# Holding back the part-array products of a recurrent layer and issuing them with a step of the recurrence, sorted by shape

## The chip, the core and the metric

One core of a Trainium2 chip runs one launch of the kernel. The metric is the device time of that launch in microseconds (us), lower is better. The engines are called TensorE (PE in the rows, its weight loads PEld), VectorE (DVE), ScalarE (ACT), GpSimd (POOL) and SyncE (SP, which issues the DMAs).

## What is computed

One layer of a hybrid encoder over 512 prompt frames and 32 sample frames, 544 in all, in fp32. A normalised input goes through one input projection; sixteen heads of stick-breaking attention and sixteen heads of an RWKV-7 recurrence work on its columns; their outputs are concatenated and go through one output projection; then a gated FFN follows.

```python
proj = rms_norm(x, norm1_g) @ w_in
q, k, v, xr = split(proj)
o = rms_norm(stick_breaking(q, k, v))
y_r, S_T = rwkv7_mix(xr, shift0, S0)
x = x + concat([o, y_r]) @ w_out
x = x + conv_ffn(rms_norm(x, norm2_g))
...
def step(S, inp):
    sa = einsum('bhvk,bhk->bhv', S, -kk_t)
    S = S * w_t + sa * (kk_t * a_t) + v_t * k_t
    return S, einsum('bhvk,bhk->bhv', S, r_t)
```

## The kernel before

Heads are worked in pairs: a pair's two 64-wide heads lie on the 128 partitions. There are 8 pairs of recurrence heads (blocks 8 to 15 of the output projection's input) and 8 pairs of attention heads (blocks 0 to 7).

**Main products.** `project` and `part` multiply the input, split into a high and a low fp32r part (`xh`, `xl`), by weights that are split likewise after their DMA (`wr` raw, `wh` and `wl` split). For one block of 128 rows that is six matmuls of 128x272, issued by `products` (L376) into a PSUM tile `pj`, of which there are two. A column block of the input projection is 96 such matmuls. I call these the full products; they fill the array.

**Side work.** Everything of the heads runs as Python generators ("threads") that are stepped while the program is recorded. `products` calls `tick` (L130) three times per block; `tick` steps each thread whose `wake` is not past the model's clock `clk["PE"]`; a thread issues a few instructions and yields. `charge` (L75) keeps the model's clock of each engine in ns, from a fixed cost and a cost per column. The clock only decides the order in which instructions are recorded; on the chip each engine runs its own list in order and waits by semaphores. `until` (L141) advances the clock by 100 at a time with nothing issued on TensorE but side work, until a condition holds. `get` and `gets` hand out buffers; for a PSUM bank (`ps`, four of them) a thread may take one before it is free in the model and then yields until it is.

**Part-array products.** Many products of the side work use a part of the array: 64 or 32 rows, or 64 or 32 columns of it. In `rwkv` (L761) these are the decay gates (`sigms`, 64 rows), the chunk products `ps<-AR,TH` (64x128), the block inverse (64x64 and 32x32). In `rwkv_chain` (L944) they are the recurrence itself: for each pair 8 steps, each of three products that depend on each other through a copy or a multiply-add on ScalarE or VectorE:

```python
mm(q[R[h], ...], AM[h][:, c, 0:C], XV[h][:, c, 0, :], ...)   # ps<-XV,AM  128x64
mm(q[R[h], ...], c3(MI)[R[h], c, :], ru[R[h], ...], ...)     # ps<-ru,w   64x64
mm(q[R[h], ...], BK[:, c, R[h]], XV[h][:, c, 1, :], ...)     # ps<-XV,BK  128x64
```

After the last step follow the output products (64x64 and 128x64, `ps<-AR,XV` and `ps<-AM,XV`), a normalisation, the gate, and `deliver` (L692), which splits the result for the output projection or parks it in DRAM (`ocat`). A pair's chain cannot start before the one before has given back `XV` and `BK`, of which there is one each.

**Output projection.** After the last input column block, the loop `while m in OUT` (L1525) makes output column blocks while heads are still being worked. The first takes its input blocks in the order `EARLY` (L1522):

```python
EARLY = [[8, 9, 10, 11], [0, 1, 2, 3], [12, 13, 4, 5]]
...
until(lambda: all(k in oh for k in g))
part(ps, oh, ol, g, ...)
```

so its third group needs the recurrence pairs 4 and 5 (blocks 12 and 13). A block made before all heads are done is parked (`part_out`, L1503) and finished later. When all threads are done (L1551) the side buffers are given back and the FFN's buffers `q` take their place; the residual rows and the rest of the weights are loaded into them.

Of the kernel before, what the change touches and what calls it, by code (L numbers as in the profile page):

```python
# [41 lines left out]
def hymba_step(ctx: ExitStack, tc: tile.TileContext, A: dict, O: dict):  # L42
# [21 lines left out]
    clk = {e: 0.0 for e in COST}  # L64
    threads = []
    cur = [None]

    class Thread:
        def __init__(self, g, first):
            self.g, self.first, self.wake, self.rd = g, first, clk["PE"], {}  # L70

# [54 lines left out]
    def spawn(g, first=False):  # L126
        n = sum(th.first for th in threads)
        threads.insert(n if first else len(threads), Thread(g, first))

    def tick():  # L130
        for th in list(threads):
            if th.wake <= clk["PE"]:
                cur[0] = th
                try:
                    next(th.g)
                    th.wake = th.ready()
                except StopIteration:
                    threads.remove(th)
                cur[0] = None

# [30 lines left out]
    FREE = {}  # L171
    POOLS = {}
# [17 lines left out]
    def gets(tag, n, dtype=F32):  # L190
        while len(FREE[tag]) < n:
            yield
        ts = [alloc(tag, POOLS[tag][2], dtype) for _ in range(n)]
        yield from settle()
        return ts

    def getm(tag, shape=None, dtype=F32):
# [506 lines left out]
    def sigms(p, S, lw2):  # L704
        names = ("w0", "a0")
        bias = [par[name][:, p:p + 1] for name in names]
        ems = []
        for _ in names:
            x = yield from gets("w", 2)
            ems.append(x)  # L710
        for s in HALVES:
            qs = yield from gets("ps", 2)
            for q, r in zip(qs, R):
                mm(q[:, :HT], lw2[r, :], lin[r, s], True, True)
            yield
            for q, b, (e, m) in zip(qs, bias, ems):
                act(e[:, s], q[:, :HT], AF.Abs, bias=b)
                V.tensor_scalar(m[:, s], q[:, :HT], b, 0.0, op0=ALU.add, op1=ALU.min)
            put(*qs)
        yield  # L720
        spawn(sigm(S, "a0", *ems[1]))
        yield from sigm(S, "w0", *ems[0])
# [38 lines left out]
    def rwkv(p, S):  # L761
# [60 lines left out]
        for c0 in range(0, NC_, 4):  # L822
            n = min(4, NC_ - c0)
            qs = yield from gets("ps", 2)
            for c in range(n):
# [74 lines left out]
        for a_, b_ in CH:  # L900
            q = yield from get("ps")
            v, s = prod(q, NA, MT, a_, b_)
            yield
            AC.copy(GA[:, s], v)
            put(q)
        put(NA)
        for a_, b_ in CH:
            yield
            q = yield from get("ps")
            v, s = prod(q, GA, M, a_, b_)  # L910
# [9 lines left out]
        E_ = [slice(64 * h + 32, 64 * h + 64) for h in range(2)]  # L920
        q = yield from get("ps")
        q3 = q[:, 0:NC_ * 32].rearrange("p (c t) -> p c t", t=32)
# [8 lines left out]
        yield  # L931
        q = yield from get("ps")
        q3 = q[:, 0:NC_ * 32].rearrange("p (c t) -> p c t", t=32)
# [10 lines left out]
    def rwkv_chain(p, S):  # L944
# [52 lines left out]

        q = yield from get("ps")
        tr(q[:, :64], stin[0:64, :], ident[0:64, 0:64])
# [7 lines left out]
        for i in range(8):  # L1007
# [4 lines left out]
            yield  # L1012
            q = yield from get("ps")
            for u, c in enumerate(cl):
# [6 lines left out]
            yield  # L1021
            q = yield from get("ps")
            for u, c in enumerate(cl):
# [7 lines left out]
            yield  # L1031
            q = yield from get("ps")
            for u, c in enumerate(cl):
# [13 lines left out]
        for a, b in [(0, 5), (5, 9)]:  # L1047
            q = yield from get("ps")

# [12 lines left out]

        q = yield from get("ps")
        for u in range(2):
# [216 lines left out]
    def attn_sample(p, S, D):  # L1281
# [43 lines left out]
        yield  # L1325
        q = yield from get("ps")
        for h in range(2):
# [1028 lines left out]
```

## Time and profile before

| what | value |
|---|---|
| median of 3 runs | 2681.56 us (2681.29 to 2681.99) |
| profiled execution | 2680.7 us, its span 2679.0 us |
| TensorE busy | 2644.4 us, 99% of the span |
| VectorE, ScalarE, GpSimd busy | 73%, 50%, 9% |
| granted clock of TensorE, mean | 0.998 |

A busy TensorE here is one with a matmul under way; a matmul's end is modelled and overlaps the next one, so costs are read from the distance between starts, not from durations. The heads are worked in the first 1120 us, the FFN takes the rest.

### The profile page before, as it was taken

Reading aid. Unit: us, or ns where it says so; the run is one execution under the profiler, and the core shown is the slowest. Engines: PE = TensorE matmul, PEld = TensorE weight load, DVE = VectorE, ACT = ScalarE, POOL = GpSimd, SP = SyncE. Lnnn points to the kernel's source line nnn. Section 1 sums busy time; section 2 is a strip of 40 time slices with the busy share of each in tenths; the row PEclk is TensorE's granted clock in tenths of the full one; section 3 lists DMA queues with packets and bytes.
Section 4 is the critical chain, followed back from the end, with each engine's and each line's share of the span. In section 5 each row is a group of like instructions: output and inputs, shape, how many; then the busy total and the mean of one; then the engine's idle time right before and its main releaser. Section 6 shows DMA issues by size and latency. Waiting matters only on the chain.

```text
span 2679.0 us, 54701 instructions
## 1 busy us (share of the span) xinstructions
PE 2644.4 (99%) x21978; PEld 2524.2 (94%) x21978; DVE 1968.8 (73%) x3573; ACT 1345.0 (50%) x2632; POOL 238.7 (9%) x609
## 2 busy tenths in 40 slices
PE   8999999999999999999999999999999999999999
PEld 7988898888888888999999999999999999999998
DVE  6676776667666754446878888887888887787887
ACT  5555665666656465434544444444444454343443
POOL 3210110101011100021010101001010100000000
PEclk9999999999999999999999999999999999999999
DMA  5222222222222243462354333434434364565653
GB/s 193 85 69 62 77 66 75 59 79 66 67 68 75 68 121 94 132 209 73 114 136 112 104 112 108 124 113 117 112 103 120 107 204 141 166 206 151 197 164 90
DMA packets 492968, 304.01 MB, mean 113 GB/s; under 512 B 45290, under 2 KB 458346, under 8 KB 492714
## 3 DMA queue, kind: packets, MB, share of 16 engines
q1 hardware_dynamic: 491434, 296.06, 38.3%
q8 instruction: 172, 2.82, 0.4%
q0 software_dynamic: 1280, 4.46, 0.4%
q14 instruction: 82, 0.67, 0.1%
HBM read 253.30 MB, written 47.16 MB: 112 GB/s over the span
## 4 chain that ended last, share of the span: by engine, by line
PE 93%; DVE 4%; ACT 2%; issue 1%; DMA 1%; SPq 0%; DVEq 0%; ACTq 0%
PE ps L216 35%; PE pj L216 29%; PE pt L216 27%; PE ps L220 1%; DVE w L109 1%; DVE q L109 1%; ACT w L109 1%; DVE wl L109 1%; ACT wh L109 0%; DMA xr<-in_x_prompt 0%; DVE sp L109 0%; ACT sp L109 0%; DVE xl L109 0%; DVE TH L109 0%; SPq L124 0%
## 5 line engine op out<-in xcount | busy, mean ns | idle before, releaser
L216 PE MATMUL pj<-xh,wh 128*128 128x272 f32 x1846 | 535.7, 305 | 9.0 <-ACT wh L109 4.4
L216 PE MATMUL pj<-xl,wh 128*128 128x272 f32 x1846 | 505.5, 289 | 0.3 <-DVE xl L109 0.3
L109 DVE TENSOR_TENSOR q<-q,q 128x1024 f32<-128x1024 f32 (+7 forms) x466 | 473.1, 1036 | 5.8 <-ACT q L109 2.7
L216 PE MATMUL pj<-xh,wl 128*128 128x272 f32 x1846 | 434.9, 306 | 5.9 <-DVE wl L109 5.9
L216 PEld LDWEIGHTS pj<-xh,wh 128*128 128x128 f32 x1846 | 349.6, 189 | 25.2 <-ACT wh L109 5.9
L216 PEld LDWEIGHTS pj<-xl,wh 128*128 128x128 f32 x1846 | 349.5, 189 | 4.1 <-issue 1.7
L109 DVE TENSOR_TENSOR wl<-wr,wh 128x512 fp32r<-128x512 f32 (+2 forms) x299 | 212.9, 714 | 184.5 <-ACT wh L109 176.7
L109 ACT CAST wr<-q 128x512 fp32r<-128x512 f32 (+1 forms) x301 | 180.9, 614 | 306.6 <-DVE q L109 217.3
L216 PEld LDWEIGHTS pj<-xh,wl 128*128 128x128 f32 x1846 | 298.0, 189 | 26.2 <-DVE wl L109 8.4
L109 ACT CAST wh<-wr 128x512 fp32r<-128x512 f32 (+2 forms) x299 | 181.6, 610 | 189.0 <-PE pj L216 95.4
L216 PE MATMUL ps<-xh,q 128*128 128x272 f32 x922 | 241.2, 289 | 0.0
L216 PE MATMUL ps<-q,q 128*128 128x272 f32 x1160 | 237.5, 289 | 0.0
L216 PE MATMUL pt<-xh,q 128*128 128x272 f32 x1038 | 233.4, 288 | 0.0
L216 PE MATMUL pt<-q,q 128*128 128x272 f32 x844 | 215.7, 289 | 0.0
L109 DVE TENSOR_TENSOR q<-q,wr 128x512 fp32r<-128x512 f32 (+1 forms) x301 | 201.0, 676 | 0.5 <-ACT wr L109 0.4
L216 PEld LDWEIGHTS ps<-q,q 128*128 128x128 f32 x1160 | 180.9, 188 | 0.3 <-ACT f L109 0.3
L216 PEld LDWEIGHTS pt<-xh,q 128*128 128x128 f32 x1038 | 174.5, 188 | 0.0
L216 PEld LDWEIGHTS ps<-xh,q 128*128 128x128 f32 x922 | 165.3, 188 | 0.0
L109 ACT CAST q<-q 128x1024 fp32r<-128x1024 f32 (+5 forms) x200 | 149.4, 765 | 26.2 <-DVE q L109 20.9
L109 ACT CAST wh<-q 128x512 fp32r<-128x512 f32 (+1 forms) x190 | 114.4, 602 | 70.7 <-PE ps L216 34.0
L216 PEld LDWEIGHTS pt<-q,q 128*128 128x128 f32 x844 | 147.9, 188 | 0.0
L216 PE MATMUL pt<-xl,q 128*128 128x272 f32 x520 | 141.7, 289 | 0.0
(323 smaller groups left out, 6248.9 us busy)
## 6 DMA issues: line engine op xcount, KB each, us to landing
wr<-in_w_in SPq DMA_DIRECT2D x200, 256.0 KB
q<-in_w_ffn_up SPq DMA_DIRECT2D x84, 512.0 KB
q<-in_w_ffn_gate SPq DMA_DIRECT2D x80, 512.0 KB
q<-in_w_ffn_down SPq DMA_DIRECT2D x48, 512.0 KB
hd<-f SPq DMA_DIRECT2D x44, 272.0 KB
q<-hd SPq DMA_DIRECT2D x22, 544.0 KB
wr<-in_w_ffn_down SPq DMA_DIRECT2D x44, 256.0 KB
q<-in_w_ffn_down SPq DMA_DIRECT2D x24, 384.0 KB
```

What stands on the lines that cost most here:

```text
L109: return f(*a, **kw)
L216: nc.tensor.matmul(out, lhsT, rhs, start=start, stop=stop, skip_group_check=True)
L220: nc.tensor.transpose(out, in_, ident)
```

## The change

`get("ps")` becomes `banks_for(shape)` at thirteen places, all of part-array products. Such a thread yields the name of a shape, and `tick` does not step it with the others. The letter ahead says whether it is a step of the recurrence ("c") or not ("s"). When a "c" thread is ready, or a thread has been ready for more than `PATIENCE` = 8000 ns of the model's clock, all ready threads of this kind are stepped in one go, sorted by the rest of the name. A bank is now taken only when it is free in the model.

```diff
+    def step(th):
+        cur[0] = th
+        try:
+            th.part = next(th.g)
+            th.wake = th.ready()
+        except StopIteration:
+            threads.remove(th)
+        cur[0] = None
+
+    PATIENCE = 8000
+
     def tick():
         for th in list(threads):
-            if th.wake <= clk["PE"]:
...
+            if th.wake <= clk["PE"] and not th.part:
+                step(th)
+        small = [th for th in threads if th.part and th.wake <= clk["PE"]]
+        if any(th.part[0] == "c" or clk["PE"] > th.wake + PATIENCE for th in small):
+            for th in sorted(small, key=lambda th: th.part[1:]):
+                step(th)
...
+    def banks_for(shape, n=1):
+        while True:
+            yield shape
+            if sum(t <= clk["PE"] for t in FREE["ps"][:n]) == n:
+                return [alloc("ps", POOLS["ps"][2]) for _ in range(n)]
...
-            qs = yield from gets("ps", 2)
+            qs = yield from banks_for("s64x128", 2)
...
-            q = yield from get("ps")
+            q, = yield from banks_for("c128x64")
...
-            q = yield from get("ps")
+            q, = yield from banks_for("c64x64")
...
-        q = yield from get("ps")
+        q, = yield from banks_for("s32x32")
```

No instruction's shape changes and both programs hold the same 20283 matmuls; what moves is their order, on every engine, from the first pair on. Three places follow.

**TensorE, the last chunk product of a pair.** `pj` is a full product, `ps<-AR,TH` the chunk product (64 rows of the array), `ps<-XV,BK` the third product of a recurrence step (64 columns). Before, of pair 7:

```order
L216 MATMUL pj_11467<-xh_343,wh_11468 128x272
L216 MATMUL pj_11467<-xl_352,wh_11468 128x272
L216 MATMUL ps_11550<-AR_10925,TH_11210 128x128
L216 MATMUL ps_11551<-AR_10925,TH_11210 128x128
L216 MATMUL pj_11467<-xh_343,wh_11468 128x272
```

Now, of pair 6, behind the first step of pair 5's chain:

```order
L234 MATMUL pj_11715<-xh_11909,wl_11973 128x272
L234 MATMUL ps_12054<-XV_1684_11074,BK_10784 64x64
L234 MATMUL ps_12054<-XV_1686_11082,BK_10784 64x64
L234 MATMUL ps_12054<-XV_1684_11074,BK_10784 64x64
L234 MATMUL ps_12054<-XV_1686_11082,BK_10784 64x64
L234 MATMUL ps_12059<-AR_11075,TH_11465 128x128
L234 MATMUL ps_12060<-AR_11075,TH_11465 128x128
L234 MATMUL pj_11715<-xh_11956,wh_11972 128x272
```

The chunk product stood alone between full products; now it stands behind a step of the recurrence, in the same gap of the full products.

**TensorE, the first output column block.** `XV,AM`, `ru,w` and `XV,BK` are the three products of a step. Before, the chain under way is that of pair 7, the last one:

```order
L216 MATMUL pj_12825<-xh_12644,wh_12834 128x272
L216 MATMUL pj_12825<-xl_12645,wh_12834 128x272
L216 MATMUL ps_12922<-XV_1918_12142,AM_1784_11369 64x64
L216 MATMUL ps_12922<-XV_1919_12143,AM_1793_11423 64x64
L216 MATMUL pj_12825<-xh_12644,wh_12834 128x272
L216 MATMUL pj_12825<-xl_12645,wh_12834 128x272
L216 MATMUL pj_12825<-xh_12644,wl_12835 128x272 x2
```

Now it is that of pair 5, and ahead of the block's third group there are no full products:

```order
L234 MATMUL pj_11715<-xh_11956,wl_11973 128x272 x2
L234 MATMUL ps_12081<-XV_1684_11074,AM_1534_10196 64x64
L234 MATMUL ps_12081<-XV_1686_11082,AM_1542_10230 64x64
L234 MATMUL ps_12093<-ru_12085,w_11157 64x64 x2
L234 MATMUL ps_12102<-XV_1684_11074,BK_10784 64x64
L234 MATMUL ps_12102<-XV_1686_11082,BK_10784 64x64
L234 MATMUL ps_12109<-XV_1684_11074,AM_1534_10196 64x64
L234 MATMUL ps_12109<-XV_1686_11082,AM_1542_10230 64x64
```

The chain's products follow each other without a full product between them; 297 matmuls of the side work stand here before the next `pj` row.

**VectorE, the same place.** `XV` rows are the chain's copies and multiply-adds, `sp` and `w` other side work, `wl` the split of the next weights. Before:

```order
L109 TENSOR_TENSOR wl_12835<-wr_12832,wh_12834 128x512
L109 SCALAR_TENSOR_TENSOR XV_1918_12142<-XV_1918_12142,pc_10921,ps_12815 64x64
L109 SCALAR_TENSOR_TENSOR XV_1919_12143<-XV_1919_12143,pc_10921,ps_12815 64x64
L109 COPY ts_12798<-ps_12823 128x128
L109 TENSOR_TENSOR wl_12899<-wr_12838,wh_12898 128x512
L109 TENSOR_TENSOR AM_2060_12907<-w_11476,AM_2060_12907 64x512
L109 COPY w_12936<-ps_12873 52x128
```

Now:

```order
L109 COPY XV_1686_11082<-ps_12185 64x64
L109 TENSOR_TENSOR w_12165<-w_12149,w_12117 128x2x15
L109 TENSOR_TENSOR w_12117<-w_12117,w_12165 128x2x15
L109 TENSOR_TENSOR w_12165<-w_12149,w_12117 128x4x14
L109 TENSOR_TENSOR w_12117<-w_12117,w_12165 128x4x14
L109 TENSOR_TENSOR w_12165<-w_12149,w_12117 128x6x13
L109 TENSOR_TENSOR w_12117<-w_12117,w_12165 128x6x13
L109 TENSOR_TENSOR w_12124<-w_12124,w_12123 128x544
L109 TENSOR_TENSOR w_12126<-w_12126,w_12125 128x544
L109 SCALAR_TENSOR_TENSOR XV_1684_11074<-XV_1684_11074,pc_9625,ps_12205 64x64
```

The triangular solve of pair 6 (`w_12117`, thirty such instructions) and the decay gates of pair 7 stand between the chain's own instructions, and no weight split does.

## Rows read from the trace of the kernel before

**Rows 1.** The page, parts 1 and 2: busy time, and TensorE over 40 slices
```profile
PE 2644.4 (99%) x21978; PEld 2524.2 (94%) x21978; DVE 1968.8 (73%) x3573; ACT 1345.0 (50%) x2632; POOL 238.7 (9%) x609
PE   8999999999999999999999999999999999999999
PEclk9999999999999999999999999999999999999999
```
**Rows 2.** The page, part 4: the chain that ended last, by engine
```profile
PE 93%; DVE 4%; ACT 2%; issue 1%; DMA 1%; SPq 0%; DVEq 0%; ACTq 0%
```
**Rows 3.** The chain of waits in order of time: start, us, what, matmuls
```profile
1119.28 95.70 PE pj L216 x762
```
**Rows 4.** Timeline of TensorE, two recurrence products: start, us, engine, line, tiles, form, count
```profile
911.58 0.28 PE L216 MATMUL pj<-xl,wh 128*128 128x272 f32 x1
911.80 0.34 PE L216 MATMUL ps<-XV,AM 128*64 128x64 f32 x4
912.06 0.39 PE L216 MATMUL pj<-xh,wh 128*128 128x272 f32 x1
912.29 0.29 PE L216 MATMUL pj<-xl,wh 128*128 128x272 f32 x1
912.42 0.29 PE L216 MATMUL pj<-xh,wl 128*128 128x272 f32 x1
...
187.31 0.29 PE L216 MATMUL pj<-xl,wh 128*128 128x272 f32 x1
187.53 0.45 PE L216 MATMUL ps<-XV,BK 128*64 128x64 f32 x8
187.91 0.52 PE L216 MATMUL pj<-xh,wl 128*128 128x272 f32 x2
188.27 0.29 PE L216 MATMUL pj<-xh,wh 128*128 128x272 f32 x1
```
**Rows 5.** Timeline of TensorE: two shapes directly behind each other
```profile
482.31 0.29 PE L216 MATMUL pj<-xl,wh 128*128 128x272 f32 x1
482.53 0.68 PE L216 MATMUL ps<-AR,XV 64*64 64x64 f32 x16
483.14 0.69 PE L216 MATMUL ps<-AM,XV 128*64 128x64 f32 x16
```
**Rows 6.** The tile ru: min/median/max ns, first and last start
```profile
L109 ACT COPY ru<-ps x64: 193/213/268, 180.2 to 1074.6; 128x64 f32<-128x64 f32 x56, 128x128 f32<-128x128 f32 x8
```
**Rows 7.** Windows: length, busy us (instructions) by engine, PEclk, DMA share, GB/s
```profile
80.00:1120.00 1040.00, 1024.87 (x9195) 914.12 (x9195) 684.49 (x1468) 613.93 (x1352) 113.75 (x288) 1.00 0.27 77
320.00:360.00 40.00, 38.40 (x306) 34.26 (x303) 34.84 (x84) 23.30 (x57) 4.92 (x15) 1.00 0.29 83
```
**Rows 8.** Windows of the full products alone (tile pj, TensorE)
```profile
80.00:1120.00 1040.00, 781.42 (x5033) 1.00 0.27 77
```
**Rows 9.** Timeline of SP's queue where the side work ends
```profile
1125.50 0.88 SPq L124 DMA_DIRECT2D q<-xd  x2
1126.43 0.91 SPq L124 DMA_DIRECT2D q<-pd  x2
1131.30 0.95 SPq L124 DMA_DIRECT2D q<-in_w_out  x2
```
**Rows 10.** Timeline of ScalarE: the first weights of the new buffers
```profile
1135.98 0.62 ACT L109 CAST q<-q 128x512 fp32r<-128x512 f32 x1
```
**Rows 11.** Windows at the kernel's start
```profile
15.00:20.00 5.00, 3.42 (x23) 2.42 (x22) 4.50 (x11) 4.00 (x9) 0.00 (x0) 1.00 0.49 144
20.00:25.00 5.00, 2.93 (x14) 2.07 (x12) 4.17 (x8) 1.95 (x4) 4.63 (x9) 0.68 0.62 209
25.00:30.00 5.00, 4.56 (x18) 4.14 (x19) 4.89 (x8) 3.45 (x7) 3.33 (x7) 0.50 1.04 368
```
**Rows 12.** Timeline of TensorE there
```profile
23.69 0.43 PE L216 MATMUL pj<-xh,wh 128*128 128x272 f32 x1
23.91 0.43 PE L216 MATMUL pj<-xl,wh 128*128 128x272 f32 x1
```

More of the change, by code (lines that the diff above doesn't have):

```diff
@@ L69, in __init__ @@
         def __init__(self, g, first):
-            self.g, self.first, self.wake, self.rd = g, first, clk["PE"], {}
+            self.g, self.first, self.wake, self.rd, self.part = g, first, clk["PE"], {}, None
         def ready(self):
@@ L128, in spawn @@
         threads.insert(n if first else len(threads), Thread(g, first))
+    def step(th):
[7 more added lines that the diff above has]
+    PATIENCE = 8000
     def tick():
         for th in list(threads):
-            if th.wake <= clk["PE"]:
[L133 to L139, printed above, removed]
+            if th.wake <= clk["PE"] and not th.part:
[4 more added lines that the diff above has]
+                step(th)
     def until(cond):
@@ L823, in rwkv @@
             n = min(4, NC_ - c0)
-            qs = yield from gets("ps", 2)
+            qs = yield from banks_for("s64x128", 2)
             for c in range(n):
@@ L900, in rwkv @@
         for a_, b_ in CH:
-            q = yield from get("ps")
+            q, = yield from banks_for("s64x64")
             v, s = prod(q, NA, MT, a_, b_)
@@ L908, in rwkv @@
             yield
-            q = yield from get("ps")
+            q, = yield from banks_for("s64x64")
             v, s = prod(q, GA, M, a_, b_)
@@ L931, in rwkv @@
         yield
-        q = yield from get("ps")
+        q, = yield from banks_for("s32x32")
         q3 = q[:, 0:NC_ * 32].rearrange("p (c t) -> p c t", t=32)
@@ L996, in rwkv_chain @@
         put(vx)
-        q = yield from get("ps")
+        q, = yield from banks_for("s64x128")
         tr(q[:, :64], stin[0:64, :], ident[0:64, 0:64])
@@ L1012, in rwkv_chain @@
             yield
-            q = yield from get("ps")
+            q, = yield from banks_for("c128x64")
             for u, c in enumerate(cl):
@@ L1021, in rwkv_chain @@
             yield
-            q = yield from get("ps")
+            q, = yield from banks_for("c64x64")
             for u, c in enumerate(cl):
@@ L1031, in rwkv_chain @@
             yield
-            q = yield from get("ps")
+            q, = yield from banks_for("c128x64")
             for u, c in enumerate(cl):
@@ L1047, in rwkv_chain @@
         for a, b in [(0, 5), (5, 9)]:
-            q = yield from get("ps")
+            q, = yield from banks_for("s64x64")
             out = lambda h, c: q[R[h], (c - a) * C:(c - a + 1) * C]
@@ L1061, in rwkv_chain @@
         put(*XV_)
-        q = yield from get("ps")
+        q, = yield from banks_for("s128x64")
         for u in range(2):
@@ L1325, in attn_sample @@
         yield
-        q = yield from get("ps")
+        q, = yield from banks_for("s128x64")
         for h in range(2):
```

## The prediction

> **What bounds the kernel now.** I read the page first [rows 1]: TensorE is busy 99% of the span, its digit is 9 in every slice but the first, and the clock is granted in full. The chain that ended last lies on TensorE for 93% [rows 2]. So time is won where TensorE's own list gets shorter, and lost wherever its next instruction has to wait. Then I read the timeline for what one matmul and one visit to a part of the array cost, and the windows for how much room the other engines have.
>
> A full product costs its distance to the next start: 762 of them in 95.70 us, 0.126 us each [rows 3]. A visit to a part of the array costs more than its own products. From the full product at 911.58 to the second full one behind the visit, 912.29, there is 0.71 us; two full products would take 0.25, so four records of a recurrence product cost 0.46 us. The same with eight records: 187.31 to the second full one behind, which stands 0.126 ahead of 188.27, is 0.83 us, less 0.25 is 0.58 [rows 4]. Four more records cost 0.12, that is 0.03 each, and the visit itself costs 0.46 - 4 x 0.03 = **0.34 us**. A change from one shape to another inside a visit: sixteen 64x64 records take from 482.53 to 483.14, 0.61 us, and 16 x 0.03 is 0.48, so the change costs **0.13 us** [rows 5].
>
> **What the change takes away.** I count in the two orders. Before, products on a part of the array stand in 325 places between full ones, now in 260: 65 visits less. Inside the visits the shape changes 27 times before and 79 times now, 52 more. So TensorE's list gets shorter by 65 x 0.34 - 52 x 0.13 = 22.1 - 6.8 = **15 us**. All of that is on the path, TensorE being the bound. Bounds: 22 us if a change of shape were free, 4 us if it cost a whole visit (65 x 0.34 - 52 x 0.34); I take 15, since the row of two shapes is such a change itself. Both programs hold the same matmuls, so nothing else on TensorE changes.
>
> **What it moves.** A product that isn't a recurrence step now waits for one, or for 8000 ns of the model's clock. The ones ahead of a pair's first step (gates, three chunk products, six of the inverse) often find no chain under way, and those behind the last step find none either, so each may wait. The order shows how this adds up: the last step of pair 0's chain stood behind 1346 full products and now behind 1854, that of pair 4 behind 3359 and now 4505, and the chain of pair 5 begins only 4 matmuls ahead of the first output column block, where before pair 7's was under way. The recurrence is nearly two pairs late. In the trace the chains fill most of 180 to 1075 us [rows 6], so this isn't made good.
>
> It is paid at the first output column block, whose third group needs pairs 4 and 5. TensorE's list there holds 101 matmuls of the side work between the last input product and the first output product, then 48 full products with 17 others, and then 297 matmuls of the side work with no full product, because none is ready: pair 5's chain but for its first step, its output, normalisation and gate, and four steps of pair 6. Everything behind them on TensorE is queued. VectorE has 201 instructions between the same marks, ScalarE 163, GpSimd 22.
>
> How long is this stretch? In the side work VectorE takes 684.49 us for 1468 instructions, 0.466 each, and ScalarE 613.93 for 1352, 0.454 [rows 7]. So VectorE needs 201 x 0.466 = 94 us here, ScalarE 74, GpSimd 22 x 0.395 = 9. TensorE's own time: the window of 1040 us holds 5033 full products [rows 8], 634 us of it at 0.126; the other 9195 - 5033 = 4162 records took the remaining 406 us, less 15 idle, 0.094 each [rows 7]. The stretch has 723 such records, 68 us, but 31 visits less than their share (25 against 325 x 723/4162 = 56), so 68 - 31 x 0.34 = 57, and with 48 full products 63.5 us. That time has to be spent in either kernel; the loss is what the stretch takes beyond it. With VectorE never idle it is 94 - 64 = 30 us; with VectorE as busy as on the mean of the side work, 684/1040 = 66%, it is 94/0.66 - 64 = 78 us. I take its busiest stretch of 40 us, 34.84 or 87% [rows 7], since here too it has work in hand that waits for nothing but its turn: 94/0.87 - 64 = **44 us**. VectorE is the one that is late, since the solve of pair 6 and the gates of pair 7 stand between the chain's own copies.
>
> **The end of the side work.** Before, seven column blocks of the output projection are parked and finished later, now all fourteen: seven more adds of 0.7 us on VectorE, which has 34% of room, and seven more loads and stores of 0.28 MB each, beside a DMA share of 0.27 [rows 7]. But with nothing left whole, only 48 full products (6.0 us) stand between the last gate product and the first weights from the new buffers. Before, 10.5 us passed from the first residual load to the first weight's split [rows 9, 10]. I take 6 us of loss, with 0 if the loads land sooner and 15 if all sixteen residual loads queue ahead of the weights.
>
> **Other queues.** SP issues 30 DMAs in the stretch, among them the eight reloads of parked heads, which before stood among the last input products; their latency lies inside the first part of the stretch. GpSimd's 9 us hide beside VectorE's 94.
>
> **Sum.** The profiled execution is 2680.7 us, 0.9 below the median. 2680.7 - 15 + 44 + 6 = 2715.7, and against the median 2681.56 + 35 = **2716 us**, slower by 1.3%.
>
> **The rivals.**
>
> 1. The clock falls in the stretch. At the kernel's start TensorE was busy 3.42 and 2.93 us of two windows of 5, and the granted clock went to 0.68 and then 0.50, the 1.2 GHz level, for the third, where it was busy 4.56 [rows 11]; full products then stood 0.22 us apart [rows 12]. In the stretch TensorE has 64 us of work in 108, 59%, a share like those two. If the clock is down for most of it, the part of the 64 us that lies on the path between VectorE's instructions, say a fifth, doubles, +12 us, and thirty full products behind it stand 0.1 us further apart, +3: 2716 + 15 = **2731 us**. Against it: the same share at 15 to 20 us still had the full clock. The Trainium skill, "TensorE: Matmul & The Clock Gate", section "Why this matters for your kernels", asks for no idle gaps between bursts of matmuls lest the clock go to half; by that rule this rival is what happens, by the rows alone it is open.
>
> 2. The stretch costs nothing. If VectorE and ScalarE have done enough of the stretch's work before TensorE gets there, it takes TensorE's 64 us only: 2681.56 - 15 + 3 for the end of the side work = **2670 us**, faster by 0.4%. It decides at 30 us: that much of VectorE's 94 would have to be done outside. For it: VectorE has a third of its time free [rows 7]. Against it: the stretch begins with pair 5's first step, and nearly all of its VectorE work reads products that TensorE makes in the stretch itself.
>
> 3. The chains of pairs 6 and 7 stay on the path after the stretch. In the order only 6 to 8 full products (0.8 to 1.0 us) stand between their products; if each of some 40 round trips waits 0.5 us, +20 us: **2736 us**. Against it: the trace shows 15 us of TensorE idle in 1040 with the same rule for when a step is issued [rows 7].
>
> **How the numbers follow.** The forecast (2700 to 2724) 0.5, the clock 0.22, late chains 0.12, the costless stretch 0.08, and 0.08 for a stretch near its bounds. The smallest loss is 30 - 15 = 15 us, less what a smaller end and a larger saving give, 2690; the largest, 78 - 15 + 6 = 69, gives 2750; I give 2690 to 2748, which leaves out the costless stretch and the worst of several at once. A measurement of this kernel tells 0.2%, 5 us, from no change. Faster by more than that: 0.08, the second rival; within it: 0.03; slower: 0.89.
>
> **What the profile would show.** Right: part-array visits down to 260, TensorE's total busy share down, and near 1000 us a stretch of about 100 us with hardly any `pj` products, VectorE busy over 80% and TensorE waiting for `XV`, `ru` and `w`; ahead of it full products run with fewer breaks and the time at their 4800th is earlier than before. The clock rival would show 0.50 in that stretch. It would be wrong if TensorE's idle time in the first 1150 us grew by less than 20 us, or if VectorE's share in the stretch stayed near 66%.

## The result and the profile after

The change takes 2810.5 us (median of 5 runs, 2809.5 to 2818.8) against 2681.6 before: a ratio of 1.0487, 95% interval 1.0472 to 1.0502. The forecast was 2716 us, range 2690 to 2748. The direction was right; the loss is 129 us where 34 was forecast.

The page after, with the lines that answer to [rows 1]: busy time by engine, TensorE and its clock over 40 slices of 70 us.

```profile
PE 2689.1 (96%) x21978; PEld 2557.4 (91%) x21978; DVE 1973.1 (70%) x3584; ACT 1348.8 (48%) x2636; POOL 236.0 (8%) x609
PE   8999999999899967998999999999999999999999
PEclk9999999999999976999999999999999999999999
```

TensorE does the same number of matmuls, is 3% of the span idle more, and yet is busy 45 us longer: some of them ran at half clock. The dip stands in the slices from 983 to 1123 us. The windows, as in [rows 7] (length, busy us and count of TensorE, its weight loads, VectorE, ScalarE, GpSimd, then the granted clock and the DMAs):

```profile
80.00:988.00 908.00, 863.87 (x7403) 781.86 (x7402) 539.68 (x1137) 511.68 (x1104) 95.70 (x261) 0.98 0.24 69
720.00:760.00 40.00, 32.05 (x290) 26.52 (x289) 24.19 (x64) 21.43 (x44) 1.65 (x8) 0.83 0.12 34
988.00:1024.00 36.00, 25.61 (x254) 20.27 (x253) 22.76 (x45) 21.99 (x45) 1.63 (x5) 0.86 0.45 133
1024.00:1060.00 36.00, 19.70 (x100) 12.64 (x98) 28.77 (x76) 16.91 (x42) 4.65 (x5) 0.61 0.00 0
1060.00:1100.00 40.00, 30.72 (x300) 22.36 (x299) 20.87 (x42) 22.75 (x51) 5.88 (x12) 0.71 0.05 12
1100.00:1127.00 27.00, 21.93 (x129) 14.53 (x127) 20.64 (x44) 10.67 (x27) 3.79 (x2) 0.56 0.04 12
1127.00:1281.00 154.00, 153.97 (x1414) 143.53 (x1415) 63.96 (x146) 43.05 (x98) 0.29 (x2) 0.98 0.35 110
1281.00:1320.00 39.00, 28.23 (x213) 27.27 (x212) 13.18 (x23) 10.57 (x21) 0.56 (x1) 0.90 0.48 144
```

Three places lose time. In the input projection (80 to 988) TensorE is idle for 44 us of 908; before it was 15 of 1040. In the stretch at the first output column block (988 to 1127) it is busy for 98 of 139, at a granted clock of 0.56 to 0.86. At 1281 to 1320 it is idle for 11. Between the last two nothing is lost.

The steps of the chains run later, as the tile `ru` tells ([rows 6] has 180.2 to 1074.6):

```profile
L109 ACT COPY ru<-ps x64: 193/212/272, 254.2 to 1247.2; 128x64 f32<-128x64 f32 x56, 128x128 f32<-128x128 f32 x8
```

The waits of TensorE, whole run: who waited, for whom, us in all, times, longest. First before, then after.

```profile
PE pj L216 <- ACT wh L109: 4.4, 6, 1.3
PE pj L216 <- ACT w L109: 2.4, 1, 2.4
PE ps L216 <- DVE XV L109: 2.0, 3, 0.9
```
```profile
PE pj L234 <- ACT wh L109: 20.0, 3, 10.7
PE ps L234 <- DVE XV L109: 16.3, 12, 2.8
PE pj L234 <- ACT w L109: 14.8, 11, 2.4
```

The third of these is the one the prediction did not see: a full product into `pj` that waits for ScalarE to copy the block before out of that `pj`, into a tile `w`. The waits for `XV` are the recurrence's own, most of them with no full product left to cover them.

**Where the time went.** I set the trace beside the program's order and priced the order as the prediction did (0.126 us a full product, 0.34 a visit, 0.03 a record; but 0.16 for a change of shape, where it had 0.13, and the other products by their columns). What a piece of the order took beyond its price I call its loss, in us. "Middle" is full products 200 to 4799, "block" is up to the 4849th (the first output column block), "end" the rest. What a row lacks of its profiled span, 27 to 29 us, lies ahead of the 200th. The runs are told below.

| kernel | TensorE's list | middle | block | end |
|---|---|---|---|---|
| before | 2622.4 | 18.9 | 1.9 | 7.3 |
| the change, 8000 ns | 2608.6 | 72.2 | 75.6 | 23.8 |
| no patience | 2623.1 | 20.4 | 2.1 | 3.8 |
| 1000 ns | 2619.9 | 13.9 | 11.1 | 5.9 |
| 4000 ns | 2616.1 | 46.7 | 47.2 | 13.6 |
| only under a chain, 8000 | 2617.6 | 14.5 | 0.6 | 10.2 |
| only under a chain, 4000 | 2616.8 | 14.3 | 2.3 | 6.1 |
| two early groups | 2606.9 | 72.0 | 15.0 | 59.5 |
| before, 16 buffers w | 2621.4 | 40.2 | 16.6 | 3.6 |
| before, one vx | 2619.8 | 20.0 | 0.8 | 5.4 |
| unsorted | 2614.2 | 81.4 | 44.5 | 43.3 |
| ends of a chain at once | 2611.5 | 51.0 | 30.6 | 56.0 |
| preparation at once | 2619.4 | 13.6 | 20.5 | 18.5 |

The change against before: -13.8 for the list, +53.3 in the middle, +73.7 at the block, +16.5 at the end, 129.7; the two profiled spans differ by 129.8 (2808.8 and 2679.0).

### The profile page after: what moved, and what is told of

Its sections match the earlier page's. It is cut to its first block, busy times and chain, and to the rows that moved or that the text cites. A ratio compares the mean times of both kernels' runs of the same rounds, so it can differ in the third digit from the quotient of the medians.

```text
span 2808.8 us, 54741 instructions
## 1 busy us (share of the span) xinstructions
PE 2689.1 (96%) x21978; PEld 2557.4 (91%) x21978; DVE 1973.1 (70%) x3584; ACT 1348.8 (48%) x2636; POOL 236.0 (8%) x609
## 4 chain that ended last, share of the span: by engine, by line
PE 64%; DVE 3%; ACT 2%; DMA 1%; issue 1%; SPq 0%; DVEq 0%; ACTq 0%
PE ps L234 27%; PE pt L234 26%; PE pj L234 10%; DVE w L109 2%; DVE q L109 1%; ACT w L109 1%; PE ps L238 1%; DMA wr<-in_w_out 0%; DVE sp L109 0%; DVE XV L109 0%; ACT sp L109 0%; ACT f L109 0%; DMA q<-in_w_out 0%; SPq L124 0%; DVE wl L109 0%
## 5 line engine op out<-in xcount | busy, mean ns | idle before, releaser
L234 PE MATMUL pj<-xh,wh 128*128 128x272 f32 x2012 | 582.2, 304 | 43.2 <-ACT wh L109 20.0
L234 PE MATMUL pj<-xl,wh 128*128 128x272 f32 x2012 | 555.7, 292 | 0.3 <-DVE xl L109 0.3
L234 PE MATMUL pj<-xh,wl 128*128 128x272 f32 x2012 | 465.9, 305 | 2.8 <-DVE wl L109 2.5
L109 DVE TENSOR_TENSOR q<-q,q 128x1024 f32<-128x1024 f32 (+9 forms) x451 | 461.3, 1042 | 5.9 <-ACT q L109 2.6
L234 PEld LDWEIGHTS pj<-xh,wh 128*128 128x128 f32 x2012 | 386.0, 192 | 60.8 <-ACT wh L109 21.1
L234 PEld LDWEIGHTS pj<-xl,wh 128*128 128x128 f32 x2012 | 386.1, 192 | 3.2 <-DVE xl L109 0.9
L234 PEld LDWEIGHTS pj<-xh,wl 128*128 128x128 f32 x2012 | 326.8, 191 | 18.8 <-DVE wl L109 4.5
L109 ACT CAST wh<-wr 128x512 fp32r<-128x512 f32 (+2 forms) x318 | 194.7, 613 | 270.3 <-PE pj L234 185.3
L109 ACT CAST q<-q 128x1024 fp32r<-128x1024 f32 (+6 forms) x185 | 138.3, 762 | 21.6 <-DVE q L109 18.5
L109 ACT ACTIVATE w<-w 128x544 f32<-128x544 f32 (+3 forms) x224 | 135.9, 617 | 17.2 <-DVE w L109 13.4
```

Of the source, the lines that this page charges most:

```text
L109: return f(*a, **kw)
L234: nc.tensor.matmul(out, lhsT, rhs, start=start, stop=stop, skip_group_check=True)
```

## The experiments

The theory H, the lateness: a held product makes its pair late; the pair's buffers stay taken; then the reader of a finished column block gets none, and the output block finds its heads unfinished. The rivals blame the grouping itself, the sort, the clock, or one kind of wait.

### Patience of -1, 1000 and 4000 ns

```diff
-    PATIENCE = 8000
+    PATIENCE = -1
```

> Only the patience is changed, from 8000 to -1 ns: a held product goes out, with all the others that are ready and sorted by shape, as soon as one is ready. The rule for the banks and the sort stay. Theory H, the lateness: what costs time is that the side work of a pair comes late, so that its buffers stay taken, the reader of a finished column block finds none of the 18 free, and TensorE waits at the start of the next block, and at the first output column block. In this order no column block waits for a buffer, the part-array visits are 327 against 324 of before, the shape changes 25 against 27, and TensorE's own list is 0.7 us longer than before: H expects 2682 us (2677 to 2688), with no loss in the middle and none at the first output block. Rival G, the grouping: bursts of side products of one shape load VectorE and ScalarE in lumps and delay the copies out of the accumulators, whatever the patience: then over 2690.

> Patience 1000 ns instead of 8000. 311 visits, 39 shape changes, TensorE's list 2.5 us shorter than before; one short run of 21 side matmuls ahead of the first output block. H, the lateness: 2681.6 - 2.5 + 0 to 6 for that run = 2682 (2677 to 2688). G, the grouping: as for no patience or worse, over 2690.

> Patience 4000 ns. 296 visits, 47 shape changes, list 6.3 us shorter than before. In the order no column block of the input projection waits for a buffer, and 241 side matmuls stand alone at 4800 full products, where after has 101 and 297. H, the lateness: no loss in the middle, and at the first output block 241/398 of the 75.6 us that after lost there, 46: 2681.6 - 6.3 + 46 + 5 for a shorter end = 2726 (2705 to 2745). Rival L, that the loss goes simply with the length of the patience, half of it: 2681.6 + 65 = 2746, with half of the middle's 53 us in place.

Measured: 2682.1 us without patience (ratio 1.0002, 0.9993 to 1.0011), 2681.3 with 1000 ns (1.0001, 0.9992 to 1.0011), 2755.7 with 4000 (1.0276, 1.0262 to 1.0290). The new rule for the banks and the sort cost nothing by themselves: the loss comes with the waiting, and not in proportion to it (0, 75 and 129 us for 1000, 4000 and 8000 ns). Without patience hardly anything is grouped (327 visits for 324), so that run does not yet clear the grouping, rival G. A run further down does: patience of 4000 ns only under a chain groups as much as 4000 ns does here (299 visits and 296), and it is faster than before. With 4000 the block lost what H said, 47 against 46, but the middle lost 28 more than before where I had expected nothing, so that the time lies above H's range and nearer rival L's 2746; what speaks against L is 1000 ns, where it would have some 16 us and there is no loss. I had misread the order: it has three starts of a column block (at 2976, 3648 and 4416 full products) where TensorE waits, with 35 and 24 side matmuls alone at the last two.

With 1000 ns the middle loses 5 us less than before and the list is 2.5 shorter; the 9 us that 21 matmuls lose at the block give it back.

### What the middle waits for

The program's own bookkeeping, as it writes the order, tells what stands still where TensorE has to wait for a free `pj`. In the change that is so at 13 starts of column blocks, from the 2592nd to the 4704th full product; before, without patience and with patience only under a chain, at none. At 12 of the 13 the reader of a pair's values (`shift_mix`) holds one of the two `pj` while it waits for a buffer `vx`, of which there are two, both kept by late pairs. Then the next block has one `pj` to itself and cannot start before that is read. At 6 of the 13 no `w` tile is free either, of 18, so that whoever needs one to read an accumulator waits as well. In the trace 11.7, 7.3 and 6.9 us are lost at 3744, 4704 and 3168 (0, 0 and 1 `w` free), where 38, 32 and 25 side matmuls stand alone, and 1.4 to 2.9 at each of eight other starts, 43 us in all of the 53. With 4000 ns there are three such waits, each with no `w` free, and at two of them a `vx` is.

The one at 3744 (TensorE, then ScalarE; in brackets the idle time and what ended it):

```profile
727.57 0.41 PE L234 MATMUL pj<-xh,wl 128*128 128x272 f32 x2
727.91 0.68 PE L234 MATMUL ps<-w,w 64*64 64x64 f32 x16
730.32 0.45 PE L234 MATMUL ps<-sp,negtri 128*128 128x384 f32 x1 [1.73 <-ACT sp L109]
733.18 0.69 PE L234 MATMUL ps<-sp,negtri 128*128 128x384 f32 x1 [2.42 <-DVE sp L109]
...
738.38 1.17 PE L234 MATMUL ps<-w,w 32*32 32x32 f32 x36
741.83 1.59 PE L234 MATMUL ps<-sp,negtri 128*128 128x512 f32 x2 [2.28 <-ACT sp L109]
743.22 0.84 PE L234 MATMUL ps<-sp,negone 128*128 128x384 f32 x2
743.86 0.43 PE L234 MATMUL pj<-xh,wh 128*128 128x272 f32 x1
```
```profile
741.80 0.62 ACT L109 ACTIVATE w<-pj 128x544 f32<-128x544 f32 x1
742.32 0.61 ACT L109 COPY w<-pj 128x544 f32<-128x544 f32 x1
```

A column block ends at 727.9. Its successor cannot start until ScalarE has copied out the `pj` it needs, from 741.8 to 742.9. Ahead of that stand products of the attention and the inverse, one round trip behind the other. The next full product starts at 743.86.

To see the same without holding anything back, the kernel before got fewer tiles `w`, and in another run one `vx` in place of two:

```diff
-    tags(sd, w=(18, W1), hs=(2, [P, HT]), ...
+    tags(sd, w=(16, W1), hs=(2, [P, HT]), ...
```

> The kernel before, with 16 buffers in place of 18 for the side work's tiles of 576 columns (tag w): nothing is held back and nothing grouped. TensorE's list is 1 us shorter (2621.4). In the order 26, 65 and 28 side matmuls now stand alone at the starts of column blocks (3168, 3840, 4416 full products) and 143 at the first output block (4800). H, that the loss in the middle comes from the buffers (the reader of a finished column block finds none free): the same loss without any hold-back; the runs of 25, 38 and 32 in after lost 6.9, 11.7 and 7.3 us, 0.27 us per matmul, so 119 x 0.27 = 32, and at the output block 143/398 x 75.6 = 27: 2681.6 - 1 + 59 = 2740 (2715 to 2760). Rival, that the middle's loss comes from the grouping or the hold-back as such: under 2690.

> The kernel before with one buffer in place of two for a pair's values (tag vx). Nothing is held back or grouped; list 2.6 us shorter (2619.8), the last steps earlier than before's (5093 against 5171). In the order the reader of a values block now stands in its wait for vx six times, for 27 to 32 us of the model, and sits on one of the two accumulators meanwhile, while w tiles are free; the next column block then has to wait for the one accumulator left to be read. H in its second form, that in the change too a late pair's vx is what blocks an accumulator (12 of its 13 waits in the input projection): each such start waits 1.4 to 3 us, as at some 12 starts in the change: 2681.4 - 2.6 + 6 x 1.4 to 3 = 2690 (2686 to 2698), with TensorE's waits of pj for ScalarE's w or vx up from 2.4 to 8 to 16 us. Rival, that only w tiles matter, since one accumulator left is enough: 2679 (2676 to 2682).

Measured with 16 `w`: 2713.1 us, ratio 1.0119 (1.0103 to 1.0136). The sign of it is there, as TensorE's waits show:

```profile
PE pj L216 <- ACT w L109: 14.3, 6, 5.2
```
```profile
791.51 0.45 PE L216 MATMUL ps<-XV,AM 128*64 128x64 f32 x8
794.42 0.59 PE L216 MATMUL pj<-xh,wh 128*128 128x272 f32 x1 [2.46 <-ACT w L109]
```

14.3 us where the change has 14.8 and before 2.4; the middle lost 21 us more than before and the block 15. So a lack of `w` tiles alone makes TensorE wait at the starts of the blocks. The size was off, 32 us for 59 expected, just under the range: the 65 matmuls at 3840 lost 4.0 us and not 17, I think because several threads were at work in them and not one.

Measured with one `vx`: 2677.3 us, ratio 0.9980 (0.9971 to 0.9989).

```profile
PE pj L216 <- ACT w L109: 6.0, 4, 2.4
PE pj L216 <- ACT vx L109: 4.2, 2, 3.7
```

The waits came as expected, 10.2 us for 2.4, but the time is the rival's: the middle lost 20.0 us, 1.1 more than before, and the list was 2.6 shorter. An accumulator kept by a `vx` gives the short waits at the starts, and those alone are cheap; what other waits went away in return I did not separate. The long ones, as I read the orders, need that the `w` are gone too (0, 0 and 1 were free at the three). The direct test would be more buffers in the change, but there is no room for a 19th `w` or, beside 18 `w`, for a third `vx`; so how the 43 us divide between the two pools is not shown.

### Is it the third group of the first output block

```diff
-    EARLY = [[8, 9, 10, 11], [0, 1, 2, 3], [12, 13, 4, 5]]
+    EARLY = [[8, 9, 10, 11], [0, 1, 2, 3]]
```

> The change as it is, but the first output column blocks take only the groups of heads that are done anyway (8 to 11 and 0 to 3); the third group, which needs pairs 4 and 5, is left for later. TensorE's own list is 2606.9 us, 1.7 shorter than after's. Instead of 101 and 297 side matmuls alone at 4800 and 4848 full products, 101 stand at 4800 and 179 at 5784, at the end of the side work. H, the lateness: the 60.7 us lost in the 297 are saved, and the 179 cost their share of it, 179/297 x 60.7 = 37: 2810 - 1.7 - 61 + 37 = 2784 (2765 to 2800); the middle's loss of about 53 us stays. Rival, the third group alone is at fault and nothing is lost elsewhere instead: 2748. Rival, the recurrence sets the end however the output blocks are cut: 2810.

Measured: 2786.2 us (1.0395, 1.0378 to 1.0413), as H said, though not by its terms: the 60.7 us at the block are gone, but 52 came back at 5784 where 37 was expected, and the end behind it lost 3 instead of 20. The recurrence is late, and whoever needs it pays. The window of that place:

```profile
1200.00:1275.00 75.00, 46.88 (x409) 34.71 (x408) 23.55 (x58) 18.48 (x50) 0.85 (x3) 0.59 0.17 48
```

Here VectorE is busy for 31% and ScalarE for 25%. No engine is short of time; each waits for another.

### Is it the clock

```diff
             tick()
             clk["PE"] += 100
             n += 1
+            if FILL[0] is not None and n % 3 == 0:
+                nc.tensor.matmul(FILL[0][:, 0, :HT], zer, oh[8][:, :HT], start=False, stop=False, ...)
...
+            FILL[0] = ps if m == 0 and g is EARLY[2] else None
             until(lambda: all(k in oh for k in g))
```

> The change as it is, and in the stretch of 297 side matmuls at the first output column block 230 full products with zero weights are added into the same accumulator, spread over the stretch, so that TensorE isn't idle there: 230 x 0.126 = 29 us of work and 22 more visits, 7.5 us. After's stretch took 102.8 us with the clock at 0.62 to 0.74. If the half clock is what made it longer than forecast (139 us with the part ahead of it, for 108), the stretch gets shorter although TensorE has 36 us more to do: 75 to 95 us, in all 2782 to 2802. If it's the round trips between TensorE, ScalarE and VectorE, the clock rises and the stretch stays at 100 to 110: 2808 to 2818. If TensorE's own time is on the path, 139: 2847.

> The change as it is, with 138 zero-weight full products in the stretch of 297 side matmuls in place of 230: 17 us of TensorE's time, 11.5 less than with 230. With 230 the stretch took 102.5 us against 102.8 without any, at a granted clock of 0.90 against 0.64. If the round trips between the engines set its length, it stays at 101 to 104, in all 2806 to 2814. If the faster clock had won time there and the zero products in the queue had given it back, fewer of them give back less: the stretch at 92 to 98, 2796 to 2804.

The second run has `n % 5`; the weights `zer` are zero, so that the sums stay as they are. Measured: 2807.8 us with 230 zero products (ratio 1.0479, 1.0462 to 1.0496) and 2811.5 with 138 (1.0480, 1.0466 to 1.0495). From the last full product ahead of the stretch to the first behind it: 102.7 us in the change (1024.1 to 1126.9), 101.1 with 138, 102.5 with 230. The windows of the stretch, the change, 138, 230:

```profile
1024.00:1127.00 103.00, 72.36 (x524) 49.53 (x522) 70.28 (x160) 50.33 (x119) 14.31 (x19) 0.64 0.03 8
```
```profile
1024.00:1127.00 103.00, 90.02 (x669) 65.94 (x668) 72.32 (x164) 51.68 (x121) 14.06 (x19) 0.78 0.03 8
```
```profile
1024.00:1127.00 103.00, 90.62 (x756) 70.31 (x755) 71.57 (x162) 51.05 (x121) 14.83 (x20) 0.90 0.03 8
```

The clock goes from 0.64 to 0.78 and 0.90 and the length stays. The side matmuls alone (those into `ps`), in the same order:

```profile
1024.00:1127.00 103.00, 71.94 (x519) 0.64 0.03 8
```
```profile
1024.00:1127.00 103.00, 62.61 (x523) 0.78 0.03 8
```
```profile
1024.00:1127.00 103.00, 56.92 (x521) 0.90 0.03 8
```

They are busy for 15 us less, and that bought at most 1.6. Some of what the clock gives may go back where a step queues behind a zero product; but with 92 of these fewer the stretch is 1.4 us shorter, not 5 to 10. So the clock does not set the length of the stretch. What is left are its round trips, with VectorE's 70 to 72 us among them; no run shortens one of them by itself.

Behind the stretch the clock does cost something. The same 204 matmuls right behind it, first in the change, then with 230 zero products:

```profile
1126.87:1155.13 28.26, 28.26 (x204) 25.86 (x203) 18.79 (x55) 8.89 (x21) 0.07 (x1) 0.86 0.28 92
1127.20:1152.90 25.70, 25.66 (x204) 23.30 (x203) 18.51 (x54) 8.75 (x21) 0.00 (x0) 1.00 0.31 100
```

These 2.6 us are about what that run is faster by in all.

### Is it the sort, or one kind of wait

```diff
-            for th in sorted(small, key=lambda th: th.part[1:]):
+            for th in small:
```

> The change with its 8000 ns of patience, but a group goes out in the order of its threads, not sorted by shape. 282 visits and 65 changes of shape, list 5.6 us longer than after's. The sort also changes who goes first: the last steps of the pairs come later still (5894 full products for the last against 5650), side matmuls stand alone at 2592 (59), 3168 (63), 3744 (52), 4320 (44) and 248 at 4848. H, the lateness: 0.27 us for each of the 218 in the middle is 59, about what after lost there (53); 248 for 398 at the output block saves 28; a later end costs 10: 2810 + 6 + 6 - 28 + 10 = 2804 (2780 to 2830). Rival, that the sort is what makes the change slow (small shapes first, the solve last): under 2750.

For the next two, the named places get their bank without waiting, as before, for instance:

```diff
-        q, = yield from banks_for("s64x128")
+        q = yield from get("ps")
         tr(q[:, :64], stin[0:64, :], ident[0:64, 0:64])
```

> The change with 8000 ns, but the product ahead of a pair's first step (the transposed state) and the two groups behind its last step (y) don't wait; all other side products do. These three stand between one pair's use of the single XV and BK buffers and the next pair's. 272 visits, 69 changes, list 11 us shorter than before's. The last step of the last pair is behind 5916 full products (after 5650, before 5171); 33 side matmuls stand alone at 4320, 113 at 4848 and 80 at 5916. H, the lateness: 33 at 0.27 is 9, 113/398 of 75.6 is 21, the 80 at the end 15 and a short end 20: 2681.4 - 11 + 65 = 2735 (2715 to 2760). Rival, that these three waits are what makes the pairs late: 2675 or less.

> The change with 8000 ns, but everything ahead of a pair's first step is issued at once; only what stands behind the last step (y, the state's transposes) and the samples' attention waits. 316 visits, 25 changes, list 3 us shorter than before's. The last steps are 100 to 700 full products behind before's (4580 against 3904 for the sixth pair, 5372 against 5171 for the last), and 31 side matmuls stand alone at 4848. H, the lateness, is small here: 2681.4 - 3 + 31/398 of 75.6 (6) + 3 = 2687 (2679 to 2700). Rival, that what waits behind the chain is what costs: over 2740.

Measured: unsorted 2815.5 us (1.0499, 1.0483 to 1.0515), so the sort is not what makes it slow. With the ends of a chain at once 2777.4 (1.0355, 1.0341 to 1.0369): better than the change by 33 us, above H's range and far from the rival's 2675; what still waits, the preparation above all, makes the pairs late. I had put it at 2735: the end lost 56, where 80 matmuls stand alone behind the 5915th full product (33 us) and then, with every block parked, little is left to cover the weights' loads. With the preparation at once 2701.4 (1.0075, 1.0061 to 1.0089), just above H's range and far below the rival's: what waits behind the chain costs 20 us by itself: 19 more than before at the block and 11 at the end, less 5 in the middle and 3 of list. Both kinds of wait cost: without the preparation's the change is 109 us faster, without those at the ends of a chain 33 (the product of the example is freed in both runs).

### Holding back only where a step is near

If H is right, a product may wait where a chain is under way, because a step soon releases it, and nowhere else:

```diff
-        if any(th.part[0] == "c" or clk["PE"] > th.wake + PATIENCE for th in small):
+        if any(th.part[0] == "c" or clk["PE"] > th.wake + (PATIENCE if CHAINS[0] else 0) for th in small):
...
+        CHAINS[0] += 1
         for i in range(8):
...
         S["steps"] = True
+        CHAINS[0] -= 1
```

> Patience 8000 ns only while some pair's recurrence steps are under way, none otherwise: a product is held only where a step will soon come that releases it. 300 visits, 48 shape changes, list 4.8 us shorter than before; in the order no column block waits for a buffer and nothing stands alone at the first output block; the last steps of the pairs are 95 full products behind before at the end (5266 against 5171), 12 us of it. H, the lateness: the gain of the list comes through, 2681.6 - 4.8 = 2677 (2672 to 2684). G, the grouping: the 48 shape changes and the bursts cost, over 2688.

> As the run with patience only under a chain, with 4000 ns for 8000. 299 visits, 45 shape changes, list 0.8 us shorter than with 8000; the last steps of the last pair stand behind 5129 full products (5266 there, 5171 before); one place where 42 side matmuls stand between two full products (3650). H, the lateness: 2671 to 2674, as there. Rival, that a patience shorter than the time between two steps of a chain breaks groups up and gives the gain back: 2678 to 2682.

> As the run with patience only under a chain, but 750 ns of patience where no chain is under way. 300 visits, 46 shape changes, list 5.1 us shorter than before's; the last steps of the last pair stand behind 5150 full products (before 5171), nothing stands alone at the output block. H, the lateness: at least as good as with none there, 2672 (2668 to 2677), since the list is as short and the end is 116 full products earlier. Rival: any wait outside a chain costs buffers: over 2678.

> As the run with patience only under a chain (8000 ns, else none), but a group goes out in the order of its threads. 306 visits, 40 shape changes, list 0.8 us longer than with the sort. If the sort's worth is the list alone: 2674 (2670 to 2678). If it matters who goes first, because the sort puts small shapes ahead of the pairs' own order: off by over 4 us to either side.

Measured: 2672.9 us with 8000 ns, ratio 0.9966 (0.9955 to 0.9978); 2671.3 with 4000, 0.9956 (0.9943 to 0.9970); 2674.7 with 750 ns outside a chain, 0.9975 (0.9965 to 0.9985). All three beat the kernel before, by 7 to 11 us, and the change by over 130; their intervals overlap, so 750 ns outside a chain gain nothing that shows. They are H's kernels: visits fall (299 with 4000 ns, before 324 by the same count), nothing stands alone at the block, no column block waits for a buffer. TensorE's waits with 4000 ns, and its line of the page:

```profile
PE pj L235 <- ACT wh L109: 4.0, 5, 1.9
PE pj L235 <- ACT w L109: 2.4, 1, 2.4
```
```profile
PE 2637.6 (99%) x21978; PEld 2523.4 (95%) x21978; DVE 1968.4 (74%) x3573; ACT 1340.0 (50%) x2631; POOL 239.5 (9%) x609
```

The gain is about twice what the shorter list gives (5.6 us): the middle loses 14.3 us instead of 18.9. Which waits went away there I did not separate.

Unsorted it is 2678.8, 0.9990 (0.9981 to 0.9999): the sort is worth 6 us here, not the 0.8 of the list. In the table (list 2618.4, middle 17.5, block 7.4, end 7.4) the largest part of it is lost at the block.

## Why the prediction was wrong

**The shorter list, -15 us: right.** With 0.16 for a change of shape it is 13.8 (65 x 0.34 - 52 x 0.16). That the prices hold in the change is seen from 1127 to 1281 us, where TensorE is busy for 153.97 of 154 and the priced order comes out within 4 us.

**"It is paid at the first output column block": this step failed.** The prediction saw the chains come nearly two pairs late and let lateness cost nothing until someone needs the heads. But a late pair keeps its buffers, of which there are 18 `w` and two `vx` for everybody, and the reader of a finished column block needs one or two of them before TensorE can use its accumulator again. 53 of the 129 us were lost before the first output block, 43 of them at such starts, and the term was left out, not mis-sized. The run with 16 `w` shows the mechanism without any hold-back; with patience only under a chain, when pairs are not late, the loss is gone. What the prediction had in hand to find it: `getm("pj")` waits while nothing but side work is issued, and the changed order shows side matmuls alone at 3168, 3744 and 4704 full products.

**The stretch, +44 us: mis-sized, 74 measured.** Both amounts of work were right: VectorE 94 us forecast, 93.0 measured (22.8 from 988 to 1024 and 70.3 from 1024 to 1127), TensorE 64 forecast, 63 by the priced order. What failed is the step "I take its busiest stretch of 40 us, 34.84 or 87%". VectorE was busy for 93 of 138.7 us, 67%, the mean share of the side work that the prediction had as its upper bound (66%, +78) and as a sign of being wrong. The 87% came from a stretch of the input projection, where other pairs' work fills VectorE's gaps, as I read it; here there is one chain, its tail and part of the next, and VectorE waits for ScalarE and TensorE in turn:

```profile
DVE w L109 <- ACT w L109: 11.3, 6, 3.4
DVE XV L109 <- ACT XV L109: 6.2, 5, 3.1
DVE sp L109 <- ACT sp L109: 5.2, 4, 3.3
```

Where the list is a chain, a sum of busy times divided by a share is only a guess at the number of round trips.

One wait in the 74 us is of another kind. The prediction let the reloads of the parked heads hide in the first part of the stretch ("Other queues"). There TensorE is done with its side matmuls at 1004.9 and idle for 7.4 us until the first output weights are split; before, it is 1.0 at that place. SyncE issued the loads of these weights behind ten reloads (TensorE, then SyncE's queue), and until 1011.4 ScalarE splits the reloaded heads:

```profile
1012.28 0.60 PE L234 MATMUL pj<-xh,wh 128*128 128x272 f32 x1 [7.40 <-ACT wh L109]
```
```profile
999.34 5.79 SPq L124 DMA_DIRECT2D w<-ocat  x10
1005.18 9.01 SPq L124 DMA_DIRECT2D wr<-in_w_out  x6
```

**The end, +6 us: mis-sized, 16 measured.** The place and the kind of wait were right, the cover was not. After the last product of the gates TensorE waits for the first split weights, which wait for their DMA (ScalarE, TensorE, then SyncE's queue):

```profile
1318.06 0.62 ACT L109 CAST wh<-wr 128x512 fp32r<-128x512 f32 x1 [8.87 <-DMA wr<-in_w_out]
```
```profile
1318.73 0.60 PE L234 MATMUL pj<-xh,wh 128*128 128x272 f32 x1 [10.70 <-ACT wh L109]
```
```profile
1311.38 1.74 SPq L124 DMA_DIRECT2D q<-pd  x4
1313.17 1.97 SPq L124 DMA_DIRECT2D wr<-in_w_out  x4
```

The 48 full products that were to cover the loads stand behind this wait, not ahead of it: the loads of their own weights (`wr`) were issued behind the first residual loads (`q<-pd`). The wait alone is 10.7 us. Behind it, from 1332 to 1346, six waits for the split of later weights on VectorE (`pj` for `q`, 4.6 us in all) make up most of the rest.

**The rivals.** The clock fell as the first rival had it, to 0.56 to 0.71 in the stretch. The Trainium skill, "TensorE: Matmul & The Clock Gate", section "Why this matters for your kernels", asks for no idle gaps lest that happen; the trace agrees on the clock. But of its 12 us in the stretch nothing came, since raising the clock left the length as it was; its 3 us behind the stretch did, 2.6 by the run with 230 zero products. The rival was right in what it saw and wrong in most of what it charged. The costless stretch did not come. The late chains of pairs 6 and 7 cost nothing from 1127 to 1281.

The range missed because its ends bounded the sizes of the terms that the prediction had, and the largest error was a term that it did not have.

## What to carry to other kernels

When work is held back to be issued together, ask first what it holds while it waits: here two small pools of buffers, through which late side threads stopped the main stream. Hold only where something that is already under way will release it soon. And where one dependent chain is left alone, count its round trips; neither the busiest engine's work nor the clock tells how long it takes.

## What the runs showed of the hardware

Products with zero weights between the steps raised the granted clock of a stretch full of idle time from 0.64 to 0.90 and took the side matmuls' busy time from 72 to 57 us, and the stretch stayed as long (102.7 and 102.5 us). The same clock was worth 2.6 us of 28.3 right behind it, where 204 matmuls follow each other without a wait. And what is lost at matmuls that stand alone is no constant for each: 4.0 us for 65 in the kernel with 16 `w`, 11.7 for 38 at the 3744th full product of the change, 52 for 179 with two early groups, 0.06 to 0.31 us each. How many threads had work then explains the difference, as I read the orders; no run varied that alone.
